# Modulation row sums of a two-layer transformer block: their tiles, their engines and their place in the program are changed

## The chip, the core and the metric

The kernel runs on one core of a Trainium2 chip. Five engines run side by side, each in the order of its own instruction list, and wait for one another through semaphores: TensorE (PE, with its weight loads as PEld), VectorE (DVE), ScalarE (ACT), GpSimd (POOL) and SyncE (SP), whose list here consists of DMA issues. The metric is the device time of one execution in microseconds (us). Three runs of the kernel before gave 1490.27, 1490.37 and 1492.56 us; the median is 1490.37 us. The profiled execution took 1494.0 us, of which 1492.2 us are the span from its first to its last instruction.

## What is computed

Two layers run over 256 latent tokens ("x") and 256 context tokens ("ctx"); the last layer needs its context tokens only up to the attention. All is float32 and the width is 1024.

```python
c_act, cc_act = silu(c), silu(c_ctx)
for i in range(2):
    need_ctx = i < 1
    mod  = (c_act  @ w_mod[i] + b_mod[i]).reshape(6, 1024)     # for x
    modc = (cc_act @ w_mod[i] + b_mod[i]).reshape(6, 1024)     # for ctx
    h  = rms_norm(x,  norm1_g[i]) * (1 + mod[1])  + mod[0]
    hc = rms_norm(xc, norm1_g[i]) * (1 + modc[1]) + modc[0]
    # four attention branches from h @ w_in and hc @ w_in
    x  = x + mod[2] * (sum_i sigmoid(h @ w_gate[i]) * (branch[i] @ w_branch[i])) @ w_out
    h2 = rms_norm(x, norm2_g[i]) * (1 + mod[4]) + mod[3]
    u  = depthwise_conv3(h2 @ w_up)                            # 2 * 2816 columns
    x  = x + mod[5] * (silu(u[:, :2816]) * u[:, 2816:]) @ w_down
    if need_ctx: the same for xc with modc
```

`mod` and `modc` are row sums: each of the 6 x 1024 outputs of a layer is the sum over 1024 products of a column of `w_mod` with the activated conditioning vector.

## The kernel before

Activations lie with their 1024 features as 8 blocks on the 128 partitions and tokens along the free dimension: columns 0 to 255 are x, 256 to 511 are context. Every float32 weight tile of 128 x 1024 is loaded from DRAM into a tile `raw` (pool `wraw`, 4 buffers, line 264), rounded on ScalarE to `wh` (line 272), and VectorE subtracts to get the remainder `wl` (`lo_of`, a call of the helper `tt`, so it shows as line 257). A product then takes three matmuls, high by high, high by low and low by high (lines 278 to 280, `mm3`). `wh` and `wl` have 4 buffers each.

A modulation column block (`mods`, the function the change rewrites) takes one such `raw` tile, with 128 outputs on the partitions and the 1024 inputs along the free dimension. `cact` holds the activated conditioning vectors on all partitions, 1024 for x and 1024 for the context. VectorE multiplies and sums in one instruction, once for x and once for the context; the product goes to `junk`, the sum to one column of `M`:

```python
V.scalar_tensor_tensor(out=junk, in0=r, scalar=1.0, in1=cact[:, st_], op0=ALU.mult,
                       op1=ALU.mult, accum_out=M[:, 8 * m + c, st_:st_ + 1])
```

In the profile this is line 335, `junk<-raw,cact`, with a short read of the accumulator after it. There are 48 such tiles with two sums (128 outputs each) and 32 with one: parts 2, 4, 3, 5 of layer 0, parts 1, 0 of layer 1 with both, parts 2 to 5 of layer 1 with x alone. The first two parts of layer 0 are made on TensorE.

`drive` runs several generators in turn, by the share of steps each has done, so it fixes the order in which the program is written. The framework's scheduler then reorders each engine's list by what is ready in its own reckoning; the list that results is fixed in the built program. The row sums are written beside the last attention, the last merge, the output projection and the MLP of layer 0.

After the attentions of layer 0 come, in this order: the fourth `merge` (gate products, then `y` grows by a GpSimd addition `y<-y,t` for each of 8 column blocks, line 257), a split of `y` into `yh` and `yl`, and the output projection `acc<-yh,wh`, which adds into the residual `xt` on VectorE (`xt<-acc,m`, line 254). Its last blocks are done for x first and then for the context. `stats` squares on ScalarE and sums on VectorE (`ss<-ss,t`). `rstd` brings the sums to the partitions with TensorE (line 387), makes `v` on VectorE (line 389), takes the power -0.5 on GpSimd (`r<-v,mhalf`, line 257 through `pow_mhalf`) and broadcasts with TensorE (line 393). `modulate` makes `t` on VectorE, `hh` on ScalarE (line 408) and `hl` on VectorE (line 254) for each of 8 blocks and two token halves. This norm stands between the output projection and the MLP. The MLP runs 22 pairs of up products (a gate block and a value block): ScalarE and two VectorE instructions make the convolution `u` from the product in PSUM (lines 1056 and 254), and `up_act` makes the activation `ah`, `al` of each pair. After the tenth pair comes the first third of the down product.

Of the kernel before, what the change touches and what calls it, by code (L numbers as in the profile page):

```python
# [10 lines left out]
F32 = mybir.dt.float32  # L11
F32R = mybir.dt.float32r
AF = mybir.ActivationFunctionType
ALU = mybir.AluOpType
# [3 lines left out]
L, D, S, CL = 2, 1024, 256, 256  # L18
T = S + CL
P = 128  # L20
KD = D // P
# [22 lines left out]
MOD_GROUPS = [(1, 0), (2, 4), (3, 5)]  # L44
# [19 lines left out]
KIDX = {k: i for i, k in enumerate(KEYS)}  # L64
# [50 lines left out]
SM = {}  # L115
# [116 lines left out]
def backbone(ctx: ExitStack, tc, wb, xT, cc, cb, sm, rg, bias, cst, out):  # L232
    nc = tc.nc
# [3 lines left out]
    wraw = pool("wraw", 4)  # L237
# [10 lines left out]
    V, A, G = nc.vector, nc.scalar, nc.gpsimd  # L248

    def spool(es, name, bufs, **k):  # L250
        return es.enter_context(tc.tile_pool(name=name, bufs=bufs, reuse_waits="tile", **k))
# [4 lines left out]
    def tt(e, out, a, b, op):  # L256
        e.tensor_tensor(out=out, in0=a, in1=b, op=op)  # L257

    def lo_of(lo, full, hi):
        tt(V, lo, full, hi.bitcast(F32), ALU.subtract)  # L260

    def wraw_load(l, key, n=1024):
        r = wraw.tile([P, 1024], F32, name="raw")
        nc.sync.dma_start(out=r[:, :n], in_=wb[l, KIDX[key], :, :n])
        return r
# [16 lines left out]
    def drive(*gens):  # L282

        live = [[g, n, 0] for g, n in gens]
        while live:
            e = min(live, key=lambda e: (e[2] + 0.5) / e[1])
            try:
                next(e[0])
                e[2] += 1
            except StopIteration:  # L290
                live.remove(e)

    def chain(*gens):
        for g in gens:
            yield from g
# [18 lines left out]
    smts, Ms = {}, {}  # L314
# [8 lines left out]
        tt(G, r[:, :n], v, mhalf[:, :n], ALU.pow)  # L323
        return r[:, :n]

    def mods(l, *ms):

        M, smt = Ms[l], smts[l]
        for m in ms:
            n = 1 if l == L - 1 and m > 1 else 2  # L330
            g = [g for g in range(3) if m in MOD_GROUPS[g]][0]
            for c in range(KD):
                r = wraw_load(l, ("mod", g, c, MOD_GROUPS[g].index(m)))
                for st_ in range(n):
                    V.scalar_tensor_tensor(out=junk, in0=r, scalar=1.0, in1=cact[:, st_], op0=ALU.mult,  # L335
                                           op1=ALU.mult, accum_out=M[:, 8 * m + c, st_:st_ + 1])
                if c == KD - 1:
                    bm = smt[:, SM["bmod"][0] + 8 * m:SM["bmod"][0] + 8 * m + 8].unsqueeze(2).to_broadcast([P, 8, n])
                    tt(V, M[:, 8 * m:8 * m + 8, :n], M[:, 8 * m:8 * m + 8, :n], bm, ALU.add)
                yield  # L340

    def some(gen, n):

        for _ in range(n):
            next(gen)
            yield
# [119 lines left out]
    for l in range(L):  # L466
# [409 lines left out]
        def merge(i, O):  # L876
            br = None
            for m in range(KD):
                if m % 4 == 0:
                    br = wload(l, ("br", i, m // 4), 2, 512)  # L880
                wg = wload(l, ("gate", i, m), KD, P)
                ps = acc_p.tile([P, T], F32, name="acc")
                for kt in range(KD):
                    mm3(ps[:, :TT], tuple(z[:, kt] for z in wg), (hh[:, kt, :TT], hl[:, kt, :TT]), kt == 0, kt == KD - 1)
                sg = tmp.tile([P, T], F32, name="t")
                A.activation(out=sg[:, :TT], in_=ps[:, :TT], func=AF.Tanh, scale=0.5)
                ps = acc_p.tile([P, T], F32, name="acc")
                for kt in range(2):
                    w_ = tuple(z[:, kt, (m % 4) * P:(m % 4 + 1) * P] for z in br)
                    mm3(ps[:, :TT], w_, (O[0][:, kt], O[1][:, kt]), kt == 0, kt == 1)  # L890
                if i == 0:
                    stt(y[:, m], sg[:, :TT], 1.0, ps[:, :TT], ALU.add, ALU.mult)
                else:
                    stt(sg[:, :TT], sg[:, :TT], 1.0, ps[:, :TT], ALU.add, ALU.mult)
                    tt(G, y[:, m], y[:, m], sg[:, :TT], ALU.add)
                yield
# [42 lines left out]
        for t in range(4):  # L939
# [24 lines left out]
              (merge(1, O1), 8),  # L964
              (chain(win_block(l, "mkv", A2, use_mkv), win_block(l, "mqa", qh, use_mqa), flush()), (16 + nq) * (1, 0.56)[l]))
        O1 = newO()
        mg = mods(0, 2, 4, 3, 5) if l == 0 else None
        drive((attend(PAIR, probs_ml, Vt["ml"], lambda h: 64 * h, post_plain(O1)), na), (merge(2, O), 8 * (1, 1.96)[l]),
              *([(some(mg, 6), 6)] if l == 0 else []))
        aes.close()  # L970
        if l == 0:
            drive((merge(3, O1), 8), (some(mg, 10), 10))
        else:
            drive((merge(3, O1), 8))


        if l == 0:
            xp = ctx.enter_context(tc.tile_pool(name="xt", bufs=1, reuse_waits="tile"))
            xt = xp.tile([P, KD, T], F32, name="xt")
            for h in range(2):  # L980
                nc.sync.dma_start(out=xt[:, 4 * h:4 * h + 4], in_=xT[:, 4 * h:4 * h + 4])
        yes2 = ExitStack()
        ysp = spool(yes2, f"ys{l}", 1)
        yh = ysp.tile([P, KD, TT], F32R, name="yh")
# [33 lines left out]
        def add_x(sc):  # L1018
            def f(m, p_, ps):
# [4 lines left out]
        accs = {}  # L1024
        drive((split_tail(lambda m: wload(l, ("out", m), KD, P), KD, lambda kt, sl: (yh[:, kt, sl], yl[:, kt, sl]),
                          add_x(lambda m, s: m2[:, m, s:s + 1]), accs, xt, parts), 11),
              (some(mg, 8) if l == 0 else iter(()), 13.7))
        yes2.close()
        yes.close()

# [31 lines left out]
        def up_act(f):  # L1062
            g, v = us.pop(f), us.pop(NF + f)
            A.activation(out=g[:, :TT], in_=g[:, :TT], func=AF.Silu)
            tt(V, g[:, :TT], g[:, :TT], v[:, :TT], ALU.mult)
            ah = ap_.tile([P, T], F32R, name="ah")
            al = ap_.tile([P, T], F32R, name="al")
            A.copy(ah[:, :TT], g[:, :TT])
            lo_of(al[:, :TT], g[:, :TT], ah[:, :TT])
            acts[f] = (ah, al)  # L1070

        def up_w(ff):
# [26 lines left out]
        def ffn(accs):  # L1099
            fs = 0  # L1100
            if ns > 1:
                fs = 2
                lst = [0, NF, 1, NF + 1]
                ws = [up_w(ff) for ff in lst]
                for a, b, s in parts:
                    for ff, w_ in zip(lst, ws):
                        conv(ff, up_ps(ff, w_, a, b), a, b)
                        yield
                up_act(0)
                up_act(1)  # L1110
            for f in range(fs, NF):
                for ff in (f, NF + f):
                    conv(ff, up_ps(ff, up_w(ff), 0, TT), 0, TT)
                    yield
                up_act(f)
                if f == 9:
                    yield from down(0)
            yield from down(1)
            yield from down(2, accs)

        if not last:
            small(l + 1)
            accs = {}
            drive((ffn(accs), 75), (chain(mg, mods(1, 1, 0, 2, 4, 3, 5)), 59))
        else:
            drive((ffn(None), 68))
        fes.close()
        if not last:
            bcs = accs["bc"]

# [21 lines left out]
```

## Time and profile before

| quantity | value |
|---|---|
| median of three runs | 1490.37 us |
| profiled execution, whole | 1494.0 us |
| its span | 1492.2 us |
| PE busy | 1436.2 us (96%) |
| DVE busy | 1058.1 us (71%) |
| ACT busy | 665.3 us (45%) |
| POOL busy | 207.7 us (14%) |
| mean granted TensorE clock | 0.985 of full speed |
| HBM read | 199.69 MB, 135 GB/s over the span |

The busy time of an engine holds the time in which a started instruction waits for a port. Busy shares are means over stages with different limits, so the stage has to be looked at by itself: the fourth merge lies at about 482 to 532 us of the span, the output projection for x from there to 567 us, the norm and the first four up blocks from there to 606 us, and the rest of the up products to about 900 us, with the first third of the down product among them.

### The profile page before, as it was taken

Reading aid. Unit: us, or ns where it says so; the run is one execution under the profiler, and the core shown is the slowest. Engines: PE = TensorE matmul, PEld = TensorE weight load, DVE = VectorE, ACT = ScalarE, POOL = GpSimd, SP = SyncE. Lnnn points to the kernel's source line nnn. Section 1 sums busy time; section 2 is a strip of 40 time slices with the busy share of each in tenths; the row PEclk is TensorE's granted clock in tenths of the full one; section 3 lists DMA queues with packets and bytes.
Section 4 is the critical chain, followed back from the end, with each engine's and each line's share of the span. In section 5 each row is a group of like instructions: output and inputs, shape, how many; then the busy total and the mean of one; then the engine's idle time right before and its main releaser. Section 6 shows DMA issues by size and latency. Waiting matters only on the chain.

```text
span 1492.2 us, 22332 instructions
## 1 busy us (share of the span) xinstructions
PE 1436.2 (96%) x8526; PEld 1199.4 (80%) x8526; DVE 1058.1 (71%) x1911; ACT 665.3 (45%) x1197; POOL 207.7 (14%) x191
## 2 busy tenths in 40 slices
PE   6999999999999996999999899999999999899999
PEld 4777667776777886888887678888888888899999
DVE  5666646648676889999566665668776575687884
ACT  5445533444333333543133341356555544464662
POOL 0343002214111200000000000024213231000000
PEclk9999999999999998999999999999999999999999
DMA  9421101213234554555544444423131333455553
GB/s 378 179 76 51 57 32 54 68 41 129 85 114 168 191 192 142 171 182 169 179 152 153 165 155 146 158 99 110 68 117 65 128 132 125 140 189 184 182 182 113
DMA packets 57930, 202.19 MB, mean 135 GB/s; under 512 B 6560, under 2 KB 8096, under 8 KB 57184
## 3 DMA queue, kind: packets, MB, share of 16 engines
q1 hardware_dynamic: 57824, 200.77, 39.3%
q8 instruction: 67, 1.10, 0.3%
q14 instruction: 39, 0.32, 0.1%
HBM read 199.69 MB, written 1.05 MB: 135 GB/s over the span
## 4 chain that ended last, share of the span: by engine, by line
PE 73%; DVE 9%; DMA 9%; issue 5%; ACT 2%; POOL 0%; SPq 0%; POOLq 0%; DVEq 0%; ACTq 0%
PE acc L278 20%; PE acc L279 19%; PE acc L280 19%; DMA raw<-in_wb_dram 9%; PE av L819 4%; DVE wl L257 3%; PE sc L738 3%; PE tp L811 2%; DVE junk L335 2%; PE sc L753 2%; PE sc L752 2%; DVE u L254 1%; ACT wh L272 1%; DVE t L254 1%; PE acc L714 1%
## 5 line engine op out<-in xcount | busy, mean ns | idle before, releaser
L272 ACT CAST wh<-raw 128x1024 fp32r<-128x1024 f32 (+1 forms) x272 | 279.3, 1028 | 385.8 <-PE acc L279 297.4
L278 PE MATMUL acc<-hh,wh 128*128 128x256 f32 (+1 forms) x1248 | 425.4, 342 | 21.3 <-DVE u L254 14.2
L279 PE MATMUL acc<-hl,wh 128*128 128x256 f32 (+1 forms) x1248 | 419.9, 337 | 0.6 <-DVE hl L254 0.6
L280 PE MATMUL acc<-hh,wl 128*128 128x256 f32 (+1 forms) x1248 | 419.6, 337 | 0.0
L257 DVE TENSOR_TENSOR wl<-raw,wh 128x1024 fp32r<-128x1024 f32 (+1 forms) x272 | 330.7, 1216 | 103.7 <-ACT wh L272 101.4
L278 PEld LDWEIGHTS acc<-hh,wh 128*128 128x128 f32 x1248 | 239.6, 193 | 52.6 <-issue 21.8
L279 PEld LDWEIGHTS acc<-hl,wh 128*128 128x128 f32 x1248 | 240.0, 192 | 27.1 <-issue 3.9
L280 PEld LDWEIGHTS acc<-hh,wl 128*128 128x128 f32 x1248 | 240.0, 192 | 25.6 <-issue 2.5
L335 DVE SCALAR_TENSOR_TENSOR junk<-raw,cact 128x1024 bf16<-128x1024 f32 x128 | 159.6, 1247 | 116.9 <-DMA raw<-in_wb_dram 116.4
L257 POOL TENSOR_TENSOR r<-v,mhalf 128x4 f32<-128x4 f32 (+3 forms) x59 | 83.0, 1412 | 759.2 <-DVE v L389 467.5
L278 PE MATMUL acc<-wh,hh 128*128 128x256 f32 (+3 forms) x496 | 149.6, 302 | 2.5 <-ACT hh L408 2.4
L279 PE MATMUL acc<-wl,hh 128*128 128x256 f32 (+3 forms) x496 | 148.2, 299 | 0.0
L280 PE MATMUL acc<-wh,hl 128*128 128x256 f32 (+3 forms) x496 | 145.1, 298 | 0.0
L278 PE MATMUL acc<-ah,wh 128*128 128x256 f32 (+1 forms) x370 | 121.5, 328 | 1.0 <-DVE u L254 1.0
L279 PE MATMUL acc<-al,wh 128*128 128x256 f32 (+1 forms) x370 | 121.6, 329 | 0.0
L280 PE MATMUL acc<-ah,wl 128*128 128x256 f32 (+1 forms) x370 | 121.5, 328 | 0.0
L254 DVE SCALAR_TENSOR_TENSOR u<-acc,smt,u 128x255 f32<-128x255 f32 (+1 forms) x184 | 108.5, 593 | 2.1 <-ACT u L1056 0.6
L278 PEld LDWEIGHTS acc<-wh,hh 128*128 128x128 f32 x496 | 95.6, 193 | 12.3 <-ACT hh L408 5.0
L761 ACT ACTIVATE p<-sc,nm 128x512 f32<-128x512 f32 (+1 forms) x120 | 74.2, 619 | 66.0 <-DVE nm L758 44.2
L758 DVE TENSOR_REDUCE nm<-sc 128x1 f32<-128x512 f32 (+1 forms) x120 | 71.2, 597 | 45.1 <-PE sc L753 32.6
L280 PEld LDWEIGHTS acc<-wh,hl 128*128 128x128 f32 x496 | 94.8, 192 | 9.0 <-issue 4.9
L279 PEld LDWEIGHTS acc<-wl,hh 128*128 128x128 f32 x496 | 95.6, 193 | 7.6 <-issue 5.2
(165 smaller groups left out, 2075.0 us busy)
## 6 DMA issues: line engine op xcount, KB each, us to landing
raw<-in_wb_dram SPq DMA_DIRECT2D x328, 512.0 KB, 3.3
mraw<-in_wb_dram SPq DMA_DIRECT2D x16, 512.0 KB, 10.2
raw<-in_wb_dram SPq DMA_DIRECT2D x20, 384.0 KB, 2.9
x<-in_xT_dram SPq DMA_DIRECT2D x2, 1024.0 KB, 6.3
bt<-in_bias_dram SPq DMA_DIRECT2D x8, 256.0 KB, 3.5
xt<-in_xT_dram SPq DMA_DIRECT2D x2, 1024.0 KB, 6.6
raw<-in_wb_dram SPq DMA_DIRECT2D x4, 320.0 KB, 2.7
cact<-in_cb_dram SPq DMA_DIRECT2D x1, 1024.0 KB, 11.4
```

The costliest lines, as they stand in the source:

```text
L254: V.scalar_tensor_tensor(out=out, in0=in0, scalar=scalar, in1=in1, op0=op0, op1=op1)
L257: e.tensor_tensor(out=out, in0=a, in1=b, op=op)
L272: A.copy(h[:, :w], r[:, :w])
L278: mm(ps, lhsT=a[0], rhs=b[0], start=first, stop=False)
L279: mm(ps, lhsT=a[0], rhs=b[1], start=False, stop=False)
L280: mm(ps, lhsT=a[1], rhs=b[0], start=False, stop=last)
L335: V.scalar_tensor_tensor(out=junk, in0=r, scalar=1.0, in1=cact[:, st_], op0=ALU.mult, op1=ALU.mult, accum_out=M[:, 8 * m + c, st_:st_ + 1])
L738: mm(sps[:, :n], lhsT=q[o:o + d, c:c + P], rhs=k[o:o + d, T - n:], start=True, stop=True)
L752: mm(sps[:, :n], lhsT=q[rs, 2 * i + r % 2, c:c + P], rhs=kk[rs], start=True, stop=False)
L758: V.tensor_reduce(out=nm, in_=sps[:, :n], op=ALU.max, axis=AX.X, negate=True)
L761: A.activation(out=p[:, :n], in_=sps[:, :n], func=AF.Exp, bias=nm, accum_out=s)
L819: mm(av[64 * j:64 * j + 64], lhsT=V_[:, 4 - nk + i, vcol(hd):vcol(hd) + 64], rhs=PTs[j][:, i], start=i == 0, stop=i == nk - 1, tile_positi ...
```

## The change

`mods` takes its column blocks from one list `plan`, with a pool for the tiles, an optional pool for products, and a number of tiles to load ahead. The first 6 tiles still go through `wraw` beside the last attention. The other 74 go through a pool `mr` of 4 buffers of its own, loaded two ahead. For these, where there is a context sum, GpSimd multiplies into a tile `pr` (2 buffers) and ScalarE sums it with an accumulating activation; the x sum stays on VectorE. The program's text has 12 tiles beside the fourth merge, 6 beside the output projection, none beside the first 8 steps of the MLP, and 56 beside the rest of it. In `up_act`, the product of the activation and the remainder `al` go from VectorE to GpSimd, in both layers.

```diff
-    def mods(l, *ms):
-        M, smt = Ms[l], smts[l]
-        for m in ms:
-            n = 1 if l == L - 1 and m > 1 else 2
...
-            for c in range(KD):
-                r = wraw_load(l, ("mod", g, c, MOD_GROUPS[g].index(m)))
-                for st_ in range(n):
+    plan = [(l, m, c) for l, m in [(0, 2), (0, 4), (0, 3), (0, 5), (1, 1), (1, 0), (1, 2), (1, 4), (1, 3), (1, 5)]
+            for c in range(KD)]
+    def mods(n, raws, prods=None, ahead=0):
+        todo = [plan.pop(0) for _ in range(n)]
+        got = []
+        def load():
+            l, m, c = todo[len(got)]
+            r = raws.tile([P, 1024], F32, name="raw")
...
+            nc.sync.dma_start(out=r, in_=wb[l, KIDX["mod", g, c, MOD_GROUPS[g].index(m)]])
+            got.append(r)
+        for i, (l, m, c) in enumerate(todo):
+            while len(got) < min(i + 1 + ahead, n):
+                load()
+            r, M = got[i], Ms[l]
+            ns = 1 if l == L - 1 and m > 1 else 2
+            for st_ in range(ns):
+                o = M[:, 8 * m + c, st_:st_ + 1]
+                if st_ and prods is not None:
+                    pr = prods.tile([P, 1024], F32, name="pr")
+                    tt(G, pr, r, cact[:, st_], ALU.mult)
+                    A.activation(out=pr, in_=pr, func=AF.Identity, accum_out=o)
+                else:
                     V.scalar_tensor_tensor(out=junk, in0=r, scalar=1.0, in1=cact[:, st_], op0=ALU.mult,
-                                           op1=ALU.mult, accum_out=M[:, 8 * m + c, st_:st_ + 1])
+                                           op1=ALU.mult, accum_out=o)
...
-              *([(some(mg, 6), 6)] if l == 0 else []))
+              *([(mods(6, wraw), 6)] if l == 0 else []))
         aes.close()
-        if l == 0:
-            drive((merge(3, O1), 8), (some(mg, 10), 10))
...
+            mrp = spool(mes, "mr", 4)
+            mpp = spool(mes, "mpr", 2)
+            drive((merge(3, O1), 8), (mods(12, mrp, mpp, 2), 12))
...
-              (some(mg, 8) if l == 0 else iter(()), 13.7))
+              (mods(6, mrp, mpp, 2) if l == 0 else iter(()), 15))
...
-            tt(V, g[:, :TT], g[:, :TT], v[:, :TT], ALU.mult)
+            tt(G, g[:, :TT], g[:, :TT], v[:, :TT], ALU.mult)
...
-            lo_of(al[:, :TT], g[:, :TT], ah[:, :TT])
+            tt(G, al[:, :TT], g[:, :TT], ah[:, :TT].bitcast(F32), ALU.subtract)
...
-            drive((ffn(accs), 75), (chain(mg, mods(1, 1, 0, 2, 4, 3, 5)), 59))
+            body = ffn(accs)
+            drive((some(body, 8), 8))
+            drive((body, 70), (mods(56, mrp, mpp, 2), 59))
```

What the built programs hold shows where the moved work stands. GpSimd's list before, from the end of the attentions of layer 0 to the start of layer 1 (`y` is the merged branches, of the 17 additions the last 8 belong to the fourth merge; `r` is the power of a norm, the first two of the three being those of the norm before the MLP):

```order
L257 TENSOR_TENSOR st<-st,rb 128x4x32
L257 TENSOR_TENSOR y<-y,t 128x512
L257 TENSOR_TENSOR r<-v,mhalf 128x8 x2
L257 TENSOR_TENSOR y<-y,t 128x512 x17
L257 TENSOR_TENSOR r<-v,mhalf 128x2 x3
L257 TENSOR_TENSOR bt<-bt,C 128x512
```

The same list now, from the first product of a context row sum (`pr`) on; the 7 rows of additions hold the 8 of the fourth merge:

```order
L257 TENSOR_TENSOR pr<-raw,cact 128x1024 x2
L257 TENSOR_TENSOR y<-y,t 128x512
L257 TENSOR_TENSOR pr<-raw,cact 128x1024 x2
L257 TENSOR_TENSOR y<-y,t 128x512 x2
L257 TENSOR_TENSOR pr<-raw,cact 128x1024 x3
L257 TENSOR_TENSOR y<-y,t 128x512
L257 TENSOR_TENSOR pr<-raw,cact 128x1024 x3
L257 TENSOR_TENSOR y<-y,t 128x512
...
L257 TENSOR_TENSOR pr<-raw,cact 128x1024 x15
L257 TENSOR_TENSOR r<-v,mhalf 128x2
L257 TENSOR_TENSOR pr<-raw,cact 128x1024 x5
L257 TENSOR_TENSOR r<-v,mhalf 128x2
```

The "..." passes over the last three additions of the merge, with 2, 3 and 2 products ahead of them. So 17 products stand ahead of the last addition of the merge, 15 more ahead of the first power of the norm, 5 between its two powers and 5 behind the second: all 42.

VectorE's list before, where the norm's x half begins (`v` is what the power is taken of, `t` and `hl` belong to `modulate`, `junk` is a row sum):

```order
L389 TENSOR_SCALAR v<-tp 128x2
L257 TENSOR_TENSOR ss<-ss,t 128x256
L254 SCALAR_TENSOR_TENSOR xt<-acc,m_4946,xt 128x256
L257 TENSOR_TENSOR wl<-raw,wh 128x1024
...
L335 SCALAR_TENSOR_TENSOR junk,M<-raw,cact 128x1024
L254 SCALAR_TENSOR_TENSOR t<-xt,s_5389,sc 128x256 x2
...
L335 SCALAR_TENSOR_TENSOR junk,M<-raw,cact 128x1024
L254 SCALAR_TENSOR_TENSOR hl<-t,M,hh 128x256
L254 SCALAR_TENSOR_TENSOR t<-xt,s_5389,sc 128x256
```

The same place now:

```order
L409 TENSOR_SCALAR v<-tp 128x2
L254 SCALAR_TENSOR_TENSOR xt<-acc,m_4984,xt 128x256
L257 TENSOR_TENSOR wl<-raw,wh 128x1024
L354 SCALAR_TENSOR_TENSOR junk,M<-raw,cact 128x1024
...
L254 SCALAR_TENSOR_TENSOR t<-xt,s_5431,sc 128x256 x2
L257 TENSOR_TENSOR ss<-ss,t 128x256
L354 SCALAR_TENSOR_TENSOR junk,M<-raw,cact 128x1024
L254 SCALAR_TENSOR_TENSOR hl<-t,M,hh 128x256
L254 SCALAR_TENSOR_TENSOR t<-xt,s_5431,sc 128x256
```

Row sums still stand between the steps of the norm. From the first row sum of a tile in `mr` up to `v` of the norm's x half, VectorE's list now has 32 row sums, 15 `wl`, 12 `ss`, 8 `yl`, 8 `t<-t,acc`, 14 `xt` and 8 small ones; from there to the last `hl` of the norm it has 13 row sums, 16 `hl`, 16 `t`, 6 `u`, 2 `wl`, 2 `ss`, 2 `xt` and 5 small ones. Of the row sums, 29 are left behind that point, and the load of the last of their tiles stands in SP's list before the second tile of the tenth up pair.

## Rows read from the trace of the kernel before

**Rows 1.** Page, part 1: busy us, share of the span, instructions.

```profile
PE 1436.2 (96%) x8526; PEld 1199.4 (80%) x8526; DVE 1058.1 (71%) x1911; ACT 665.3 (45%) x1197; POOL 207.7 (14%) x191
```

**Rows 2.** Windows: length, busy us by engine (instructions), granted clock, DMA share, GB/s.

```profile
482.00:532.00 50.00, 50.00 (x220) 40.96 (x219) 43.92 (x62) 15.39 (x22) 13.74 (x8) 1.00 0.61 208
532.00:567.30 35.30, 35.30 (x220) 31.95 (x220) 28.14 (x53) 13.53 (x22) 0.03 (x1) 1.00 0.49 164
567.30:606.00 38.70, 27.32 (x182) 26.47 (x182) 37.56 (x79) 13.93 (x27) 1.49 (x2) 0.78 0.39 136
606.00:770.00 164.00, 164.00 (x743) 136.27 (x742) 130.92 (x200) 60.85 (x78) 0.00 (x0) 1.00 0.53 179
770.00:905.00 135.00, 125.92 (x546) 101.52 (x545) 93.58 (x132) 48.49 (x64) 0.00 (x0) 1.00 0.47 156
```

**Rows 3.** Waits, 482 to 606 us: who for whom, us, times, longest.

```profile
PE acc L278 <- DVE u L254: 6.2, 1, 6.2
PE acc L278 <- ACT hh L408: 4.6, 1, 4.6
```

**Rows 4.** Waits, 770 to 905 us.

```profile
DVE junk L335 <- DMA raw<-in_wb_dram: 37.8, 18, 3.1
...
PE acc L278 <- DVE u L254: 7.8, 7, 1.7
...
PE acc L278 <- DVE s L257: 1.3, 1, 1.3
```

**Rows 5.** Windows of the tile junk alone: two instructions to a row sum.

```profile
0.00:482.00 482.00, 32.63 (x52) 0.99 0.31 108
482.00:567.30 85.30, 34.58 (x52) 1.00 0.56 190
567.30:606.00 38.70, 17.14 (x28) 0.78 0.39 136
606.00:905.00 299.00, 70.11 (x114) 1.00 0.50 169
```

**Rows 6.** Timeline of POOL: start, us, instruction, and idle time before it.

```profile
514.18 2.15 POOL L257 TENSOR_TENSOR y<-y,t 128x512 f32<-128x512 f32 x1 [4.80 <-DVE t L254]
522.32 1.30 POOL L257 TENSOR_TENSOR y<-y,t 128x512 f32<-128x512 f32 x1 [5.98 <-DVE t L254]
```

**Rows 7.** Timeline of DVE beside the first of these.

```profile
513.36 0.67 DVE L254 SCALAR_TENSOR_TENSOR t<-t,acc 128x512 f32<-128x512 f32 x1
513.96 1.21 DVE L335 SCALAR_TENSOR_TENSOR junk<-raw,cact 128x1024 bf16<-128x1024 f32 x1
...
515.21 2.20 DVE L335 SCALAR_TENSOR_TENSOR junk<-raw,cact 128x1024 bf16<-128x1024 f32 x1
```

**Rows 8.** Timeline of POOL, layer 1: the same addition at half the width.

```profile
1161.20 0.73 POOL L257 TENSOR_TENSOR y<-y,t 128x256 f32<-128x256 f32 x1 [2.48 <-DVE t L254]
```

**Rows 9.** DVE's groups, 482 to 567.3 us: count, busy us, mean ns, idle before.

```profile
L335 DVE SCALAR_TENSOR_TENSOR junk<-raw,cact 128x1024 bf16<-128x1024 f32 x26 | 34.4, 1321 | 9.8 <-DMA raw<-in_wb_dram 9.6
L257 DVE TENSOR_TENSOR wl<-raw,wh 128x1024 fp32r<-128x1024 f32 x15 | 18.2, 1218 | 2.9 <-ACT wh L272 2.9
L254 DVE SCALAR_TENSOR_TENSOR xt<-acc,m,xt 128x256 f32<-128x256 f32 x14 | 6.2, 477 | 0.7 <-PE acc L280 0.5
L257 DVE TENSOR_TENSOR yl<-y,yh 128x512 fp32r<-128x512 f32 x8 | 5.9, 738 | 1.6 <-ACT yh L987 1.5
...
L257 DVE TENSOR_TENSOR ss<-ss,t 128x256 f32<-128x256 f32 x12 | 4.7, 418 | 1.1 <-ACT t L375 1.1
```

**Rows 10.** DVE's groups, 567.3 to 606 us.

```profile
L254 DVE SCALAR_TENSOR_TENSOR hl<-t,M,hh 128x256 fp32r<-128x256 f32 x16 | 7.5, 476 | 0.0
```

**Rows 11.** ACT's groups over the span: a cast of this width, an accumulator read.

```profile
L272 ACT CAST wh<-raw 128x1024 fp32r<-128x1024 f32 (+1 forms) x272 | 279.3, 1028 | 385.8 <-PE acc L279 297.4 <-issue 58.8 <-PE acc L280 17.2
...
L761 ACT ACTIVATION_READ_ACCUMULATOR p<-sc,nm 128x1 f32 x120 | 23.8, 198 | 0.0
```

**Rows 12.** DVE's groups over the span: the convolution on 512 tokens.

```profile
L254 DVE SCALAR_TENSOR_TENSOR u<-acc,smt,u 128x510 f32<-128x510 f32 x80 | 59.5, 744 | 1.4 <-ACT u L1056 0.6
```

More of the change, by code (lines that the diff above doesn't have):

```diff
@@ L324, in pow_mhalf @@
         return r[:, :n]
-    def mods(l, *ms):
-        M, smt = Ms[l], smts[l]
-        for m in ms:
-            n = 1 if l == L - 1 and m > 1 else 2
-            g = [g for g in range(3) if m in MOD_GROUPS[g]][0]
-            for c in range(KD):
-                r = wraw_load(l, ("mod", g, c, MOD_GROUPS[g].index(m)))
-                for st_ in range(n):
-                    V.scalar_tensor_tensor(out=junk, in0=r, scalar=1.0, in1=cact[:, st_], op0=ALU.mult,
-                                           op1=ALU.mult, accum_out=M[:, 8 * m + c, st_:st_ + 1])
[L337 to L340, printed above, removed]
+    plan = [(l, m, c) for l, m in [(0, 2), (0, 4), (0, 3), (0, 5), (1, 1), (1, 0), (1, 2), (1, 4), (1, 3), (1, 5)]
+            for c in range(KD)]
@@ new lines, in mods @@
+    def mods(n, raws, prods=None, ahead=0):
[4 more added lines that the diff above has]
+            r = raws.tile([P, 1024], F32, name="raw")
+            g = [g for g in range(3) if m in MOD_GROUPS[g]][0]
+            nc.sync.dma_start(out=r, in_=wb[l, KIDX["mod", g, c, MOD_GROUPS[g].index(m)]])
[12 more added lines that the diff above has]
+                else:
+                    V.scalar_tensor_tensor(out=junk, in0=r, scalar=1.0, in1=cact[:, st_], op0=ALU.mult,
+                                           op1=ALU.mult, accum_out=o)
+            if c == KD - 1:
+                b0 = SM["bmod"][0] + 8 * m
+                bm = smts[l][:, b0:b0 + 8].unsqueeze(2).to_broadcast([P, 8, ns])
+                tt(V, M[:, 8 * m:8 * m + 8, :ns], M[:, 8 * m:8 * m + 8, :ns], bm, ALU.add)
+            yield
@@ L966, in backbone @@
         O1 = newO()
-        mg = mods(0, 2, 4, 3, 5) if l == 0 else None
         drive((attend(PAIR, probs_ml, Vt["ml"], lambda h: 64 * h, post_plain(O1)), na), (merge(2, O), 8 * (1, 1.96)[l]),
-              *([(some(mg, 6), 6)] if l == 0 else []))
+              *([(mods(6, wraw), 6)] if l == 0 else []))
         aes.close()
-        if l == 0:
-            drive((merge(3, O1), 8), (some(mg, 10), 10))
-        else:
-            drive((merge(3, O1), 8))
         if l == 0:
@@ L979, in backbone @@
             xt = xp.tile([P, KD, T], F32, name="xt")
+            mes = ExitStack()
+            mrp = spool(mes, "mr", 4)
+            mpp = spool(mes, "mpr", 2)
+            drive((merge(3, O1), 8), (mods(12, mrp, mpp, 2), 12))
             for h in range(2):
                 nc.sync.dma_start(out=xt[:, 4 * h:4 * h + 4], in_=xT[:, 4 * h:4 * h + 4])
+        else:
+            drive((merge(3, O1), 8))
         yes2 = ExitStack()
@@ L1127, in backbone @@
         fes.close()
+        if l == 0:
+            mes.close()
         if not last:
```

## The prediction

> **What bounds the kernel now.** I first read the page's busy times: PE is busy 1436.2 of 1492.2 us [rows 1], so a change elsewhere can win only what PE loses in waits and low clock, but can lose without limit. Then the windows by stage [rows 2]. From 482 to 567.3 us PE is busy in every microsecond. From 567.3 to 606 us, the norm ahead of the MLP, it has 27.32 of 38.70 us at a granted clock of 0.78; the waits name the convolution of the first up blocks and `hh` behind `t`, 6.2 and 4.6 us [rows 3]. VectorE is busy 37.56 of those 38.70 us, so its list sets that stage. From 606 to 770 us PE is full again. From 770 to 905 us it loses 135.00 - 125.92 = 9.1 us, in 8 short waits for VectorE of 7.8 + 1.3 us; there VectorE itself stands 37.8 us before row sums whose tile hasn't landed [rows 4].
>
> The row sums are spread out: 26 up to 482 us, 26 to 567.3, 14 in the norm, 57 to 905 us [rows 5], at two instructions to a row sum.
>
> Last, how GpSimd and VectorE get on. An addition of 128x512 takes GpSimd 1.30 us at 522.32, where VectorE has no instruction with two inputs in SBUF [rows 6]. At 514.18 it takes 2.15 us: VectorE has been in a row sum since 513.96, which ends at about 515.1. The next row sum, issued at 515.21, then takes 2.20 us instead of 1.21 and ends just 1.1 us after the addition [rows 6, 7]. Each waited for the whole of the other. VectorE's `t<-t,acc` at 513.36 kept its 0.67 us; its second input comes from PSUM. So a VectorE instruction with two SBUF inputs and a GpSimd product exclude each other.
>
> The Trainium skill has this as a rule (SBUF — State Buffer, "Who interferes with whom"): a VectorE instruction with two SBUF inputs contends with a GpSimd one that reads SBUF, and the second to issue fully blocks. The trace agrees up to 128x512, by the 0.85 us of the addition and the 1.0 us of the row sum above; no row has a product of 128x1024, and by the rule its whole length shuts VectorE out.
>
> **The change part by part.**
>
> *Price of a product.* No row shows 128x1024 on GpSimd. The same operation takes 0.73 us for 256 columns and 1.30 us for 512 [rows 6, 8]: 0.57 us per 256, so 1.30 + 2 x 0.57 = 2.44 us. Some of it is overlap of records; I take 2.4 us. Bounds: 2.2 us (a slope a fifth lower) and 2 x 1.30 = 2.6 us.
>
> The Trainium skill has an addition of 2048 columns at 4497 ns (GPSIMD Engine Reference, "Elementwise — side-by-side cycle accounting"); half of it, an estimate, is 2.25 us. By it the first stretch below would be 32 x 0.15 = 5 us shorter. No run here has shown that width yet.
>
> *Holds on VectorE.* Records overlap by about 0.08 us, so a row sum holds 1.15 us (513.96 to the 515.1 above), a `wl` 1.218 - 0.08 = 1.14, a `yl` 0.66, an `ss` 0.34, an `hl` 0.40 us [rows 7, 9, 10].
>
> *First stretch: from the first tile of the new pool to the norm's first power* (482 to 567.3 us before, 85.3 us). The pool's space comes free with the attentions, so it can't begin much earlier. By the order, VectorE must do 32 row sums, 15 `wl`, 8 `yl`, 12 `ss` and 7 small two-input ones before `v`: 36.8 + 17.1 + 5.3 + 4.1 + 0.6 = 63.9 us. GpSimd must do 32 products and 8 additions before the power: 32 x 2.4 + 8 x 1.30 = 87.2 us. Alone, that would just fit. But they exclude each other: 151.1 us, against 85.3: **+65.8 us**. Before, the same sum is 26 x 1.15 + 27.1 + 10.4 = 67 us, which fits. With products at 2.2 or 2.6 us it is +59 or +72. Nothing covers it: the last addition of the merge stands behind 17 products, and the output projection needs it whole; the power stands behind 15 more, and the up products need it. ScalarE isn't in the way: 32 accumulating activations of about 1.03 + 0.20 us are 39 us, on top of 15.39 + 13.53 busy [rows 2, 11]. The port isn't always in use either: VectorE waited 9.8 us there for landings and 2.9 for casts [rows 9]. In the new order some of that falls into GpSimd's holds: 0 to 12.7 us, I take **+3**.
>
> *Second stretch: the norm* (38.70 us before). The text puts no row sum there, but the list has 13, where the trace had 14 [rows 5]. VectorE's two-input work is 13 x 1.15 + 16 x 0.40 + 2 x 1.14 + 2 x 0.34 + 0.4 = 24.8 us, its other 24 instructions at about 0.40 us (477 ns less the overlap [rows 9]) 9.6 us. GpSimd has 10 products: 24 us. If the 9.6 us all lie under products, 48.8 us; if none do, 58.4 us: +10 to +20, and since ScalarE's `hh` stand in turn with the sums of these products, I take **+15**. PE's idle time and the low clock lie inside this stretch before and after, so they aren't counted again.
>
> *Rest of the up products.* 29 row sums are left, and they end with the tenth pair, on tiles of their own. The waits of 770 to 905 us go: **-9.1 us** (0 if something replaces them). Up to there a pair takes PE 48 matmuls x 164/743 = 10.6 us [rows 2]; VectorE has 2 `wl`, 4 `u` at 0.66 [rows 12] and 3.6 row sums, 2.3 + 2.6 + 4.2 = 9.1 us, and GpSimd's two activation instructions of 1.30 us hold it at most 2.6 us more: 11.7 us at worst. 0 to 8 x 1.1 = 9 us, I take **+2**. Later pairs and all of layer 1 have no row sums, and the two instructions are covered by the pairs that lie between an activation and the down product that reads it: 0.
>
> *Queues.* SP has 74 loads on tiles of the new pool between weight loads. They wait for products, and weight tiles behind them wait too; eight weight tiles (four raw, four split) of 24 matmuls at 0.22 us are 42 us ahead, which covers a ring of four products. I cost it at nothing beyond the stretches.
>
> *Sum:* 65.8 + 3 + 15 - 9.1 + 2 = +76.7 us. Against the profiled execution 1492.2 + 76.7 = 1569 us span, 1571 us whole; its time (1494.0 us) stood 3.6 us above the median of the runs, so **1567 us**.
>
> **The rivals.**
>
> *Products and row sums overlap after all, faster* (8%). If a product of this width doesn't shut VectorE out, GpSimd's 87.2 us almost fit into 85.3 us, the norm keeps its 13 row sums (no gain), and the 9.1 us are won: 1490 - 9 + 2 = 1483 us. It decides where VectorE's row sums beside a product stay at 1.2 us. Against it: every overlap of this form in the rows is a full wait.
>
> *Part of a product shuts VectorE out* (6%). The longest hold that the rows show is 1.30 us. With that per product, the first stretch is 63.9 + 10.4 + 41.6 = 116 us, +31; the second 24.8 + 13 = 38 us, no change: +31 + 3 - 9 + 2 = +27, 1517 us.
>
> *Nothing overlaps, and more* (7%). Also the one-input instructions stand behind holds: 8 x 0.60 + 14 x 0.40 = 10 us more in the first stretch, 12.7 for landings and casts, 20 in the norm, 9 in the up products, and weight tiles late enough that the 9.1 us don't come back: 66 + 10 + 13 + 20 + 9 = +118, 1608 us.
>
> *The order absorbs it* (3%). It would need products of (85.3 - 63.9 - 10.4) / 32 = 0.34 us, half of what 256 columns take. Within 0.2%.
>
> **How the numbers follow.** The forecast, that port times add up, has 76%: 1567 us, with its own bounds 1551 (59.4 + 0 + 10 - 9.1 + 0, products of 2.2 us) to 1595 us (72.2 + 12.7 + 20 - 9.1 + 9, of 2.6 us). 1515 to 1602 us takes in the partial hold and holds about 82%. A measurement here tells 0.2% from no change: slower 89%, same 3%, faster 8%.
>
> **What would show it.** Right: the `pr` products at 2.4 us where VectorE has nothing with two SBUF inputs, and about 3.5 us otherwise; row sums and `wl` at a mean near 2 us or more between the fourth merge and the first up blocks; the last addition `y<-y,t` some 30 us later, the first power of the norm about 65 us later; PE busy little more than half there, waiting for `yh`, then for `hh`; granted clock below full there; no waits for VectorE in the later up products. Wrong: row sums at 1.2 us beside products, PE full up to the norm, or the loss in the up products instead.

## The result, and the profile after

The changed kernel takes **1562.91 us** (median of 4 runs, 1560.92 to 1566.35) against 1490.32 us (4 runs, 1488.76 to 1492.56): a ratio of 1.0495, 95% interval 1.0472 to 1.0517. It is slower by 72.6 us; 1567 us was forecast. The profiled execution took 1563.83 us, with a span of 1562.0 us against 1492.2, so 69.8 us are to be found in the trace. Part 1 of the page, busy times as in [rows 1]:

```profile
PE 1453.5 (93%) x8526; PEld 1213.9 (78%) x8526; DVE 1070.0 (69%) x1739; ACT 710.0 (45%) x1281; POOL 450.0 (29%) x321
```

VectorE runs 172 instructions fewer and is busy 11.9 us longer: its instructions have become longer. The windows, cut at the first product on GpSimd (472.7), the last addition of the merge (554.5), the norm's first power (622.3), 4 us behind the norm's last `hl` (680), 9 us behind the last row sum (760), and behind the up products (975); length, busy time and instructions by engine, granted clock, DMA share, GB/s, as [rows 2]:

```profile
472.70:554.50 81.80, 65.14 (x246) 51.22 (x245) 80.96 (x64) 36.08 (x58) 68.42 (x24) 0.87 0.51 184
554.50:622.30 67.80, 46.21 (x235) 40.28 (x233) 67.77 (x69) 27.79 (x50) 47.92 (x16) 0.84 0.49 172
622.30:680.00 57.70, 27.89 (x148) 26.33 (x149) 57.66 (x82) 22.82 (x46) 28.47 (x12) 0.63 0.49 171
680.00:760.00 80.00, 76.53 (x356) 63.92 (x356) 76.27 (x106) 33.95 (x45) 25.35 (x14) 0.98 0.75 257
760.00:975.00 215.00, 215.00 (x950) 178.09 (x949) 100.59 (x121) 79.02 (x99) 46.56 (x30) 1.00 0.28 96
```

Where PE had been full up to the norm, it is now busy 65.14 + 46.21 = 111.4 of 149.6 us, and in the norm 27.89 of 57.70 at a granted clock of 0.63, where it was 0.78. VectorE is idle for 0.9 us in the three stretches together. From 760 us on PE is full: the 9.1 us of short waits of [rows 4] are gone. The waits of PE from 472 to 700 us (answering [rows 3]) are 70.0 us, and 50.9 of them name VectorE, with its steps in the merge (`t`), the split behind it (`yl`), the norm (`hl`) and the first up products (`u`). The rest name ScalarE's `hh` and `t` and GpSimd's power. The five longest of nine rows:

```profile
PE acc L278 <- DVE t L254: 16.7, 4, 6.5
PE acc L279 <- DVE hl L254: 11.4, 3, 4.7
PE acc L278 <- DVE u L254: 9.9, 2, 8.2
PE acc L278 <- ACT hh L428: 8.9, 1, 8.9
PE acc L279 <- DVE yl L257: 7.0, 2, 4.7
```

Why VectorE is late stands in its groups from 472.7 to 622.3 us, as [rows 9] (count, busy us, mean ns, idle before):

```profile
L354 DVE SCALAR_TENSOR_TENSOR junk<-raw,cact 128x1024 bf16<-128x1024 f32 x32 | 72.9, 2278 | 0.2
L257 DVE TENSOR_TENSOR wl<-raw,wh 128x1024 fp32r<-128x1024 f32 x16 | 37.4, 2340 | 4.2 <-ACT wh L272 4.2
L257 DVE TENSOR_TENSOR yl<-y,yh 128x512 fp32r<-128x512 f32 x8 | 14.1, 1758 | 0.0
...
L254 DVE SCALAR_TENSOR_TENSOR t<-t,acc 128x512 f32<-128x512 f32 x8 | 5.4, 675 | 0.0
```

Row sums take 2278 ns and `wl` 2340, against 1321 and 1218 in [rows 9]; `yl` 1758 against 738. (The 4.2 us of idle time in the row of `wl` lie ahead of the window, before its first one.) The `t<-t,acc`, whose second operand is in PSUM, keep the 0.67 us of [rows 7]. In the norm the 16 `hl`, at 476 ns in [rows 10], are held too (622.3 to 680 us):

```profile
L254 DVE SCALAR_TENSOR_TENSOR hl<-t,M,hh 128x256 fp32r<-128x256 f32 x16 | 15.1, 952 | 0.0
```

The timeline shows one turn of this. GpSimd, an addition and two products:

```profile
480.25 2.21 POOL L257 TENSOR_TENSOR y<-y,t 128x512 f32<-128x512 f32 x1 [1.77 <-DVE t L254]
482.43 6.72 POOL L257 TENSOR_TENSOR pr<-raw,cact 128x1024 f32<-128x1024 f32 x2
```

and VectorE beside them:

```profile
481.24 2.31 DVE L257 TENSOR_TENSOR wl<-raw,wh 128x1024 fp32r<-128x1024 f32 x1
483.47 0.68 DVE L254 SCALAR_TENSOR_TENSOR t<-t,acc 128x512 f32<-128x512 f32 x1
484.07 2.81 DVE L354 SCALAR_TENSOR_TENSOR junk<-raw,cact 128x1024 bf16<-128x1024 f32 x1
486.81 0.08 DVE L354 DVE_READ_ACCUMULATOR junk<-raw,cact 128x1 f32 x1
486.81 2.37 DVE L257 TENSOR_TENSOR M<-M,smt 128x16 f32<-128x16 f32 x1
```

`wl` waits for the addition and then runs until 483.55; the first product, there since 482.43, can only then start. Its own length is 2.34 us, by two products later on that VectorE hardly holds up:

```profile
644.61 4.67 POOL L257 TENSOR_TENSOR pr<-raw,cact 128x1024 f32<-128x1024 f32 x2 [1.27 <-ACT pr L352]
```

So it ends at 485.9. The row sum issued at 484.07 has waited for it and ends at about 486.85, where its accumulator is read. The second product follows until 489.15, and an addition of 16 columns, `M`, takes 2.37 us because it stands behind it. By this reading the two products last 1.12 + 2.34 + 0.95 + 2.34 = 6.75 us; the row says 6.72. Over the span, 42 products have a mean of 3.1 us:

```profile
L257 POOL TENSOR_TENSOR pr<-raw,cact 128x1024 f32<-128x1024 f32 x42 | 128.4, 3079 | 33.0 <-ACT pr L352 28.1 <-DMA raw<-in_wb_dram 4.8
```

The 33.0 us at its end are idle time of GpSimd ahead of products, 28.1 of them until ScalarE had summed a `pr` tile. VectorE worked on through them, so the two engines' turns, and not these waits, fill the time.

### The profile page after: what moved, and what is told of

It reads as the page before. It is cut to its first block, busy times and chain, and to the rows that moved or that the text cites. A ratio compares the mean times of both kernels' runs of the same rounds, so it can differ in the third digit from the quotient of the medians.

```text
span 1562.0 us, 22477 instructions
## 1 busy us (share of the span) xinstructions
PE 1453.5 (93%) x8526; PEld 1213.9 (78%) x8526; DVE 1070.0 (69%) x1739; ACT 710.0 (45%) x1281; POOL 450.0 (29%) x321
## 4 chain that ended last, share of the span: by engine, by line
PE 79%; DVE 11%; issue 6%; ACT 2%; DMA 1%; POOL 0%; SPq 0%; DVEq 0%; POOLq 0%; ACTq 0%
PE acc L278 22%; PE acc L279 21%; PE acc L280 21%; DVE junk L354 4%; PE av L839 3%; PE sc L758 3%; DVE wl L257 2%; PE tp L831 2%; PE sc L773 2%; PE sc L772 1%; DMA raw<-in_wb_dram 1%; DVE hl L254 1%; ACT wh L272 1%; DVE t L254 1%; DVE u L254 1%
## 5 line engine op out<-in xcount | busy, mean ns | idle before, releaser
L257 DVE TENSOR_TENSOR wl<-raw,wh 128x1024 fp32r<-128x1024 f32 (+1 forms) x272 | 353.8, 1301 | 197.6 <-ACT wh L272 195.4
L354 DVE SCALAR_TENSOR_TENSOR junk<-raw,cact 128x1024 bf16<-128x1024 f32 x86 | 150.3, 1748 | 9.4 <-DMA raw<-in_wb_dram 9.0
L257 POOL TENSOR_TENSOR u<-u,u 128x512 f32<-128x512 f32 (+1 forms) x44 | 53.6, 1218 | 301.0 <-DVE u L254 259.9
L257 POOL TENSOR_TENSOR pr<-raw,cact 128x1024 f32<-128x1024 f32 x42 | 128.4, 3079 | 33.0 <-ACT pr L352 28.1
L257 POOL TENSOR_TENSOR y<-y,t 128x512 f32<-128x512 f32 (+1 forms) x48 | 59.9, 1251 | 183.7 <-DVE t L254 162.1
```

## The experiments

**Theory 1** (the prediction's): a GpSimd product and a VectorE instruction with two operands in SBUF take turns, so that their times add; the loss is 42 products on a path that VectorE sets. **Theory 2**: GpSimd's list is merely long, and the merge's additions and the norm's powers stand in it behind products; VectorE isn't held. **Theory 3**: the own tiles, the loads two ahead and the row sums pulled earlier cost the time. **Theory 4**: the activation products do. Ratios below are to the kernel before on the same chip, with 95% intervals.

**The products replaced by fills.** The context's products are left out, so its modulation is a constant; GpSimd writes as many tiles and reads none.

```diff
-                    tt(G, pr, r, cact[:, st_], ALU.mult)
+                    for _ in range(3):
+                        G.memset(pr, 0.001)
```

> The changed kernel with each GpSimd product of the context replaced by three fills of the same tile with a constant, so that GpSimd reads nothing and only writes; the context's products are left out, and its modulation becomes a constant. 126 fills stand where 42 products stood, and ScalarE still sums each tile. If three fills are about as long as a product: theory 1 (turns on the operands' reads): VectorE's row sums beside them return to 1.2 us and the loss is mostly gone, 1485 to 1510 us. Theory 2 (a long list on GpSimd alone): still 1545 to 1565 us.

Measured: 1488.67 us, ratio 0.9987 (0.9972 to 1.0001). The fills take 0.95 us each (115.6 us for all 126, against 128.4 us for the products), ScalarE sums as many tiles as in the changed kernel, and some 80 of the 126 lie ahead of the norm's first power, in the place of 27 products (32 stood there). So the built order is near the changed kernel's, but not the same. The window from 472.7 us to that power, at 562.44 us:

```profile
472.70:562.40 89.70, 89.70 (x456) 76.38 (x455) 85.38 (x132) 57.29 (x97) 82.02 (x84) 1.00 0.87 307
```

GpSimd is busy 82.02 and VectorE 85.38 of 89.70 us at once, and PE is never idle. The timelines of GpSimd and of VectorE show a row sum that starts within three fills and takes 1.21 us:

```profile
480.33 2.74 POOL L352 MEMSET pr<- 128x1024 f32 x3
```

```profile
481.99 1.21 DVE L355 SCALAR_TENSOR_TENSOR junk<-raw,cact 128x1024 bf16<-128x1024 f32 x1
```

It isn't a lucky one. The row sums of the whole window have a mean of 1364 ns, near the 1321 of [rows 9] and far from 2278:

```profile
L355 DVE SCALAR_TENSOR_TENSOR junk<-raw,cact 128x1024 bf16<-128x1024 f32 x35 | 47.7, 1364 | 0.6 <-DMA raw<-in_wb_dram 0.4
...
L1012 DVE TENSOR_SCALAR m<-M 128x16 f32<-128x16 f32 x1 | 2.2, 2153 | 0.0
```

The second row is an exception: `m<-M`, an instruction of 16 columns with one operand, in SBUF, takes 2.15 us beside fills, 1.26 beside an addition in the changed kernel, and 0.16 where everything is on VectorE. It stands once in the stretch, so the result doesn't hang on it.

So a list nearly as long, in nearly the same places and with the same number of ScalarE's sums, costs nothing: theory 2 falls, and so does a limit in ScalarE's sums or in the two `pr` tiles. What costs is that GpSimd reads.

**The products replaced by copies**, two for each: GpSimd reads one tile instead of two. The context's products are left out here too.

```diff
-                    tt(G, pr, r, cact[:, st_], ALU.mult)
+                    for _ in range(2):
+                        G.tensor_copy(out=pr, in_=r)
```

> The changed kernel with each GpSimd product of the context replaced by two copies of the raw tile, so that GpSimd reads one tile from SBUF and not two; the context's products are left out, so its modulation has wrong numbers. 84 copies stand where 42 products stood. If two copies take about as long as a product (2 to 3 us): theory 1 in its narrow form (only an instruction with two operands in SBUF holds VectorE's two-operand ones up): VectorE's row sums stay at 1.2 to 1.4 us, and the time is 1485 to 1500 us. Theory 1 in a wider form (any read by GpSimd takes turns with them): 1540 to 1565 us. Theory 2 (the list's length) was answered by the fills.

Measured: 1513.87 us, ratio 1.0144 (1.0130 to 1.0157), between the two expectations. As a time it doesn't decide, since the built order changed with the instruction: 22 of the 84 copies stand ahead of the norm's first power (32 of the 42 products did), and PE waits 21.5 us for the norm's `hh`, behind row sums whose tiles come late. The rows decide more. GpSimd:

```profile
497.25 2.11 POOL L352 COPY pr<-raw 128x1024 f32<-128x1024 f32 x1
```

and VectorE:

```profile
497.25 1.21 DVE L257 TENSOR_TENSOR wl<-raw,wh 128x1024 fp32r<-128x1024 f32 x1
498.38 2.05 DVE L355 SCALAR_TENSOR_TENSOR junk<-raw,cact 128x1024 bf16<-128x1024 f32 x1
```

A copy alone takes 1.04 us. The one issued with the `wl` waits for it and then runs, and the row sum at 498.38 waits for the copy in turn. So one operand read by GpSimd is enough for the turns. From 472 to 700 us the 32 row sums have a mean of 1585 ns beside copies, between the 1364 of the fills' window and the 2278 of the products'.

The Trainium skill (SBUF — State Buffer, "Who interferes with whom") says that a VectorE instruction with two SBUF inputs contends with a GpSimd one that reads SBUF, and not with one that only writes it. The fills and the copies agree on both halves, by the 1.21 and the 2.05 us of these row sums.

**The context's row sums back on VectorE**, own tiles and activation products on GpSimd kept.

```diff
-                if st_ and prods is not None:
+                if False:
```

> The changed kernel with one part undone: the context's row sums are again taken by VectorE in one instruction each; own tiles, loads two ahead and the activation products on GpSimd stay. Theory 1 (a GpSimd product and a two-input VectorE instruction take turns, so that their times add): the whole loss goes, since 42 products of 2.4 us = 100 us leave GpSimd: 1480 to 1495 us. Theory 2 (GpSimd's list is merely long, the merge additions and the norm's powers stand behind its products): the same 1480 to 1495. Theory 3 (the own tiles and the row sums pulled earlier cost the time): still about 1555 to 1565.

Measured: 1497.3 us, ratio 1.0049 (1.0030 to 1.0067). 65.6 of the 72.6 us go; the time is 2.3 us above the range. Theory 3 falls as the main cause; half a per cent is left.

**The activation products back on VectorE**, all else as changed.

```diff
-            tt(G, g[:, :TT], g[:, :TT], v[:, :TT], ALU.mult)
+            tt(V, g[:, :TT], g[:, :TT], v[:, :TT], ALU.mult)
...
-            tt(G, al[:, :TT], g[:, :TT], ah[:, :TT].bitcast(F32), ALU.subtract)
+            lo_of(al[:, :TT], g[:, :TT], ah[:, :TT])
```

> The changed kernel with the two activation products of each pair in the later part of the up products back on VectorE. Theories 1 to 3: 1558 to 1568 us, no change against the changed kernel of more than 5 us, since PE waits only 1.7 us there. Theory 4 (these products on GpSimd carry the loss): 1490 to 1510.

Measured: 1558.0 us, ratio 1.0452 (1.0422 to 1.0482). Theory 4 falls as the main cause; 4.9 us by the medians may be theirs, with intervals that overlap.

**The kernel before with the context's row sums on GpSimd and ScalarE alone**: its old order, its shared raw tiles, a pool of two `pr`. The lines that make this pool, and to that end take the residual's space earlier, aren't shown.

```diff
+                    if st_ and "p" in mprod:
+                        pr = mprod["p"].tile([P, 1024], F32, name="pr")
+                        tt(G, pr, r, cact[:, st_], ALU.mult)
+                        A.activation(out=pr, in_=pr, func=AF.Identity, accum_out=o)
```

> The kernel before with one part alone: the context's row sums on GpSimd and ScalarE, in the order that the kernel before has, with its shared raw buffers; activation products on VectorE. Theories 1 and 2: slower by 45 to 90 us, 1535 to 1580, since the same 42 products lie around the merge additions and the norm. Theory 3 and theory 4: 1485 to 1500.

Measured: 1550.34 us, ratio 1.0404 (1.0373 to 1.0435). This one part makes a loss of 4% by itself. Here only 20 products lie ahead of the norm's first power, which comes at 588.17 us (+20.9); the first activation of the up products comes 34.7 us late, and the other 21 us are lost behind it. From 460 to 1000 us PE waits 26.1 us for `u` in 13 pieces, where it waited 13.9 before. VectorE's waits for tiles to land are no longer than before (103.9 for 102.6 us), so late tiles don't hold VectorE up more than they did.

**Everything on VectorE, own tiles and the new order kept**: the two edits of the first and second undoing together.

```diff
-                if st_ and prods is not None:
+                if False:
...
-            tt(G, g[:, :TT], g[:, :TT], v[:, :TT], ALU.mult)
+            tt(V, g[:, :TT], g[:, :TT], v[:, :TT], ALU.mult)
...
```

> The changed kernel with all row sums and the activation products on VectorE: only the own tiles, the loads two ahead and the order that follows from them are left of the change. The run that kept the activation products on GpSimd as well measured 1497.3 us. Theory 1: 1486 to 1497 us, the difference to the 1497.3 being what the activation products cost. Theory 3: the same 1497 or more, all of the half per cent from tiles and order.

Measured: 1486.54 us, ratio 0.9963 (0.9952 to 0.9975). Own tiles and the order that goes with them gain a little; theory 3 is wrong in sign. The two kernels that differ from it by one part price the two: the activation products on GpSimd +10.8 us (1497.3), the context's sums there +71.5 us (1558.0). These two ran on another chip than this one; by the ratios, each to the kernel before on its own chip, the prices are 0.9% and 4.9%, 13 and 73 us.

**The activation products alone**, on the kernel before.

```diff
-            tt(V, g[:, :TT], g[:, :TT], v[:, :TT], ALU.mult)
+            tt(G, g[:, :TT], g[:, :TT], v[:, :TT], ALU.mult)
...
-            lo_of(al[:, :TT], g[:, :TT], ah[:, :TT])
+            tt(G, al[:, :TT], g[:, :TT], ah[:, :TT].bitcast(F32), ALU.subtract)
```

> The kernel before with one part alone: the two activation products of each pair in the later part of the up products on GpSimd, all row sums on VectorE in their old order. Theory 1: VectorE gives up two instructions of about half a microsecond a pair and loses part of that again where its two-input instructions lie beside GpSimd's; the 9.1 us of waits there may shorten: 1483 to 1496 us. The run with these products back on VectorE measured 1558.0 us where the changed kernel has 1562.9, so if they cost by themselves what that difference says: 1493 to 1497 us.

Measured: 1506.47 us, ratio 1.0098 (1.0079 to 1.0117). A miss: two instructions of 0.69 us a pair taken off VectorE cost 1%. It is lost in the first ten pairs: from the first activation to the tenth, nine steps, they take 106.6 us, with PE busy 98.58 (430 matmuls), where before they took 92.1 with PE full (408 matmuls). Some of this is work that only moved; at the end of the span 11.6 us are left. VectorE's groups in these pairs:

```profile
L335 DVE SCALAR_TENSOR_TENSOR junk<-raw,cact 128x1024 bf16<-128x1024 f32 x29 | 40.8, 1405 | 17.5 <-DMA raw<-in_wb_dram 17.3
L257 DVE TENSOR_TENSOR wl<-raw,wh 128x1024 fp32r<-128x1024 f32 x18 | 26.9, 1496 | 0.0
```

Before, these had means of 1219 and 1218 ns, and row sums waited 5.3 us for tiles. So the holds, 29 x 0.186 + 18 x 0.278 = 10.4 us, are less than the 12.3 us that VectorE was spared; what has grown is the wait for tiles to land, by 12.0 us. Why they land later, in the ring that row sums share with the weights here, was not tested, so turns are not shown to be the whole cause of this 1%.

With own tiles VectorE doesn't wait for them. Its groups in the same pairs, of the kernel with all on VectorE first, then of the one with only the activation products on GpSimd (own tiles in both):

```profile
L354 DVE SCALAR_TENSOR_TENSOR junk<-raw,cact 128x1024 bf16<-128x1024 f32 x36 | 44.1, 1225 | 0.0
...
L257 DVE TENSOR_TENSOR wl<-raw,wh 128x1024 fp32r<-128x1024 f32 x18 | 22.1, 1229 | 1.6 <-ACT wh L272 1.5
```

```profile
L354 DVE SCALAR_TENSOR_TENSOR junk<-raw,cact 128x1024 bf16<-128x1024 f32 x44 | 60.4, 1372 | 0.1
L257 DVE TENSOR_TENSOR wl<-raw,wh 128x1024 fp32r<-128x1024 f32 x17 | 29.3, 1726 | 0.0
```

The holds give VectorE 44 x 0.147 + 17 x 0.497 = 14.9 us, more than the 18 x 0.69 = 12.4 us that it was spared. That leaves 2.5 us, where these ten pairs are 10.8 us longer (109.0 for 98.2). 8 row sums more also lie in them, about 9.8 us, and VectorE is busy 108.90 of the 109.0. Whether the pairs are longer for these row sums, or the row sums lie there because the pairs are longer, wasn't separated.

**All on VectorE, with row sums held until the norm is done.** Beside the two undoings, the first column of the vector that the sums multiply is rewritten, with its own value, by an instruction that reads the last tile of the norm; the row sums behind it wait for that. The lines stand just ahead of `drive((some(body, 8), 8))`.

```diff
+            for s_ in range(2):
+                stt(cact[:, s_, 0:1], hl[:, KD - 1, T - 1:T].bitcast(F32), 0.0, cact[:, s_, 0:1], ALU.mult, ALU.add)
```

> The changed kernel with all row sums and the activation products on VectorE, and with the row sums after the first eight made to wait for the norm's last tile (the vector that they multiply gets its first column rewritten, with the same value, by an instruction that reads that tile). Theory 1: GpSimd has no products, so the loss is gone; VectorE is free of row sums in the norm, whose 11.4 us of idle TensorE and low clock of before can shrink by 3 to 12 us, while the row sums that are held come in the up products, where each takes 1.2 us of VectorE: 1474 to 1495 us. Theory 3 (own tiles and order cost the time): 1495 or above, as the run with the context back on VectorE (1497.3).

Measured: **1471.19 us**, ratio 0.9859 (0.9842 to 0.9876), 3 us under the range that theory 1 gave, better than either kernel and 15.4 us better than the same without the hold. The windows from the norm's first power to the first activation of the up products, and from there to the tenth:

```profile
566.90:602.70 35.80, 30.23 (x239) 29.21 (x239) 33.56 (x72) 20.76 (x36) 1.57 (x2) 1.00 0.38 119
602.70:699.60 96.90, 96.90 (x429) 80.25 (x428) 95.40 (x148) 39.09 (x52) 0.00 (x0) 1.00 0.61 193
```

The last `hl` ends 20.7 us after the first power, where it was 33.2; PE keeps a granted clock of 1.00 there, against 0.78 in [rows 2]; and the row sums that were held cost nothing behind it, since PE is full. "No row sum in the norm", which the text of the change asked for, is worth these 15.4 us once the built order keeps to it; in the changed kernel's list 13 stood there.

**The held kernel with the context's sums on GpSimd again.** No product lies in the norm.

```diff
-                if False:
+                if st_ and prods is not None:
```

> The run with the held row sums (1471.2 us), with the context's 42 row sums on GpSimd and ScalarE again: no product lies in the norm; 18 stand ahead of it, between the merge additions, and 24 behind it, in the first ten pairs of the up products, where VectorE was busy for 95.4 of 96.9 us. Theory 1: the products ahead of the norm's powers delay them by about 20 to 35 us, and behind the norm 24 holds of 2.34 us (56 us) take the place of 24 sums of 1.23 us (30 us) on a full VectorE, about 15 to 35 us: 1505 to 1540 us. Theory 2 in its form that the norm's powers wait behind GpSimd's products: no product but one stands between the last merge addition and the powers, so most of the loss is gone: 1471 to 1490 us.

Measured: 1545.73 us, ratio 1.0371 (1.0353 to 1.0390); 6 us above the range of theory 1, and far from theory 2. Against the held kernel, the norm's first power is late by 31.9 us (598.82), and the ten pairs, from the first to the tenth, take 125.9 us for 96.9 (+29.0), with VectorE busy in them from end to end (the window), and with PE waiting for it (the waits, 620 to 780 us):

```profile
647.70:773.60 125.90, 104.12 (x428) 83.60 (x427) 125.90 (x146) 60.06 (x91) 52.50 (x18) 0.93 0.63 209
```

```profile
PE acc L278 <- DVE u L254: 30.3, 7, 11.1
```

The missing 13 us lie between the power and the first pair, which the expectation hadn't counted. So it isn't the norm that the products spoil but any stretch that VectorE sets.

**The held kernel with the activation products on GpSimd instead.**

```diff
-            tt(V, g[:, :TT], g[:, :TT], v[:, :TT], ALU.mult)
+            tt(G, g[:, :TT], g[:, :TT], v[:, :TT], ALU.mult)
```

(and the remainder `al` with it)

> The run with the held row sums (1471.2 us), with the two activation products of each pair on GpSimd: VectorE gives up two instructions of 0.69 us a pair and is held for two of some 1.2 us, in a stretch of ten pairs where it is full. Theory 1: ten pairs by about 1 us, 1479 to 1487 us, the same 10 to 12 us as between the two earlier runs that differ in this alone (1486.5 and 1497.3). If GpSimd relieves VectorE instead: 1458 to 1470 us.

Measured: 1483.36 us, ratio 0.9951 (0.9938 to 0.9963): +12.2 us to the held kernel by the medians, 13.7 by the ratios (the two ran on different chips), about as theory 1 expected, though the same reservation as above holds on how it comes about.

## Why the prediction was right, and where its terms were off

The mechanism is the forecast one and is now shown from both sides: with the reads of GpSimd taken away and the rest left nearly as it was, the loss is gone (fills); with the one part added to the kernel before, or to the held kernel, it is there (+4.0% and +5.2%, by 1.0371 / 0.9859). The four rivals fall by rows: row sums beside a product don't stay at 1.2 us, a product holds for the whole of its 2.34 us and not for 1.30, instructions with one operand in SBUF and one in PSUM aren't held (`t<-t,acc` at 675 ns; the small `m<-M` is the one exception seen among those with a single SBUF operand), and the order absorbs nothing. The terms, by the profiled executions:

- *Price of a product*: 2.34 us alone against the 2.4 taken, 3.3 us at the median of all 42 and 3.42 at most, against "about 3.5 us otherwise". The estimate of 2.25 us by the Trainium skill (GPSIMD Engine Reference, "Elementwise — side-by-side cycle accounting") is 4% under the 2.34 us that this trace shows.
- *First stretch*: from the first product (472.67) to the first power (622.32) 149.65 us, for a sum of 151.1; with 2.34 us a product the sum is 149.2. Adding the times of two engines gave the stretch to 0.3%. The "+3" for landings and casts wasn't there. The two rows that bound the stretch:

```profile
472.67 5.80 POOL L257 TENSOR_TENSOR pr<-raw,cact 128x1024 f32<-128x1024 f32 x2 [4.84 <-DMA raw<-in_wb_dram]
622.32 0.71 POOL L257 TENSOR_TENSOR r<-v,mhalf 128x2 f32<-128x2 f32 x1 [2.72 <-DVE v L409]
```

- *Its start* was the step that failed: "it can't begin much earlier" than 482 us. It began 9.3 us earlier, so the power came 55.0 us late and not 65.8 + 3.
- *The norm*: from the first power to the end of the last `hl` 53.5 us for 33.2, +20.3 against +15, at the upper edge of its bounds (10 to 20). VectorE's `hl` went from 476 ns [rows 10] to 952.
- From there to the first activation of the up products another 3.8 us (+79.1 in all), which the sum didn't price; with it the second stretch lies above its bounds.
- *Rest of the up products*: -9.3 us against -9.1 + 2. The first ten pairs take 2.1 us more, as forecast; the waits of [rows 4] are gone but for 1.7 us.

55.0 + 20.3 + 3.8 - 9.3 = +69.8 us. The forecast's +76.7 was 7 us too high (13.8 by the start and the "+3", and 2.2 by the rest, made up in part by the norm, +5.3 and +3.8). So 1567 us came within 4.1 us of the measured 1562.91 in part by luck: 16 us too much in some terms and 9 too little in others. The mechanism doesn't rest on that. "PE busy little more than half" up to the norm was too gloomy, at 111.4 of 149.6 us; the last addition is 24.7 us late, for 30. PE doesn't wait for `yh`, as foreseen, but for the `t` ahead of it and for `yl`.

One judgement was wrong though it hardly counted here: the activation products were put at +2 us as if GpSimd's turns were the only price. Without the context's products beside them they cost 11 to 15 us; in the changed kernel the medians say about 5, not clear of noise. What they cost beyond the turns stays open.

## What to carry to other kernels

Don't give GpSimd work that reads SBUF to relieve a VectorE that has two-operand work in SBUF to do in the same stretch: add the two engines' times, and compare the sum with the stretch. A VectorE that is "busy" throughout may be held: compare the mean of its groups with that of the same shape elsewhere. When a side job sits in a tight stage, look at the built order; making it truly wait (here by a dependence on the stage's last tile) gave 1.0% by itself and 1.4% together with own tiles, where moving it to another engine lost 5%.

## What was not expected of the hardware

- Fills of 128x1024 on GpSimd (0.95 us) ran beside two-operand row sums at 1.21 us (mean 1364 ns), and both engines were busy for over 80 of 89.70 us; one-operand copies (1.04 us) took turns with them.
- Two 0.69 us instructions a pair, moved from VectorE to a GpSimd that is idle in the up products, made the kernel slower by 11 to 13 us with own tiles and by 15 on the kernel before; on the kernel before VectorE's holds grew by less than it was spared.
- In the norm PE's granted clock was 0.63 with 27.89 of 57.70 us busy, 0.78 before with 27.32 of 38.70, and 1.00 in the held kernel with 30.23 of 35.80.
